# Router of a mixture-of-experts layer: the norm by tokens from turned blocks, its scale and shift behind the gather

## The chip, the core and the metric

The kernel runs on one core of a Trainium2 chip. The metric is device time in microseconds, the median of several runs. The engines named here are TensorE (PE), VectorE (DVE), ScalarE (ACT), GpSimd (POOL) and SyncE (SP), which issues the large weight transfers.

## The reference, cut to what matters

Two transformer blocks of two different kinds follow each other; the change lies in the first block's second layer, between its attention and its experts. There 256 tokens of width 1024 pass through:

```python
mix = jnp.concatenate([self_out, cross_out], axis=-1) @ w_out[i]
x = layer_norm(DN_ALPHA * x + mix, ln_attn_g[i], ln_attn_b[i])
ffn = moe_swiglu(x, w_router[j], b_router[j], w_exp_in[j], w_exp_out[j])
x = layer_norm(DN_ALPHA * x + ffn, ln_ffn_g[i], ln_ffn_b[i])
```

`moe_swiglu` takes `logits = x2 @ w_router + b_router`, the two largest of 8 logits for each token, a softmax of these two as gates, sends each token to its two experts (`silu(h[:, :D_FF]) * h[:, D_FF:]` between two linears) and adds the results up by the gates. `layer_norm` is `(x - mean) * rsqrt(var + eps) * g + b` over the 1024 features.

## The kernel before

Activations stand with features on the partitions: 8 blocks (`KB`) of 128 features by 256 tokens (`S`). A linear takes each weight tile from a 1 MB transfer (`raw`, issued by SP up to eight tiles ahead, five `raw` buffers and some borrowed ones); ACT makes the rounded upper part `wh` (L237), DVE the rest `wl = raw - wh` (L240), three buffers of each. Activations are split the same way (`xh`, `xl`, by `split`: ACT L218, DVE L219), and PE does three matmuls for each block of 128 by 128 weights: L285 (xh by wh), L286 (xl by wh), L287 (xh by wl). PSUM has four `acc` banks, two `pt` and two `sc`.

Each engine works its queue in the order in which the instructions stand. A tile framework's scheduler sets that order when the kernel is built: it takes what is ready by its own estimate, earlier written code first, and `tc.high_priority()` puts a piece ahead.

The second layer, in order of writing:

- `layer1` ends with the memory attention (exps L476, transposes L495, products L509, splits L218/L219). Then `residual` (L538) runs `w_out[1]`, 192 matmuls in four tiles, and evicts each of the 8 blocks on DVE as `z = alpha * x + p` (L543). `ln_mean` (L413) sums blocks on POOL and PE for the mean.
- `layer_norm` (L421): DVE subtracts the mean (L426), ACT squares (L410), PE sums the squares in 32 small matmuls (L429), `rsq` (L985 to L998) takes the inverse root on DVE, PE spreads it over the partitions (L436), DVE multiplies (L439), ACT applies scale and shift twice (L441 into `xh`, L442 into `z`), DVE makes `xl` (L444).
- `moe` (L733): starts the fetch of the first eight expert tiles, loads the router's weights `wr` on ACT's queue (`late`, L344), splits them, takes logits in 16 matmuls (L749), turns `z` into rows by tokens `xt` (transposes L758, splits L218/L219), turns the logits back (L762), picks the two experts (L768 to L785), counts positions (matmuls L789/L790, then L792/L793) and calls `gather` for the first two experts.
- `gather` (L839): one-hot matrices `oh` (L847), 32 matmuls with the upper and lower parts of `xt` into banks of their own (L854), copied out by ACT (L861, upper) and DVE (L859, lower) as `xe`, 128 by 512 each; then the turned one-hots (L868 to L873). It is called four times, the later three between expert linears.
- `expert_in` (L910 to L912) and `expert_out` run for 8 experts on tiles of 128 by 2048, then a conditional stage and the final norm.

Of the kernel before, what the change touches and what calls it, by code (L numbers as in the profile page):

```python
# [22 lines left out]
NM = 16  # L23
T2 = S + NM
# [5 lines left out]
ALPHA = 4.0 ** 0.25  # L30
# [134 lines left out]
class Kern:  # L165
# [372 lines left out]
    def residual(self, z, x, w, xs, alpha=ALPHA):  # L538
# [107 lines left out]
    def layer1(self, x, xh, xl):  # L646
        nc, I, tc = self.nc, self.i, self.tc
        with tc.tile_pool(name="l1", bufs=1) as pool:
            w = I["w_in_fox"][0]
# [10 lines left out]
            n = 0  # L660
# [53 lines left out]
        self.dbg("xa1", z)  # L714
        return z, xh, xl

    def log1p_exp_neg_abs(self, out, s, u, x):

# [11 lines left out]
        nc.vector.tensor_tensor(out, out, s, op=OP.mult)  # L730


    def moe(self, x, xh, xl):  # L733
        nc, I, tc = self.nc, self.i, self.tc
        c = self.c
        with tc.tile_pool(name="moe", bufs=1) as pool:

            raws = [None] * 5 + [self.idle(t) for t in ("xl", "xa")] + [self.pair_y(pool, F).rearrange("p a c -> p (a c)")]
# [3 lines left out]
            wr = self.late(pool, "wr")  # L742
            w2 = pool.tile([128, KB, 16], R, name="wr2")
            self.split(w2[:, :, :8], w2[:, :, 8:], wr)
            p = self.sc()[:16, :S]
            for k in range(KB):
                o = [(p, w2[:, k], xh[:, k]), (p[:8], w2[:, k, :8], xl[:, k])]
                for i, a in enumerate(o if k == 0 else o[::-1]):
                    nc.tensor.matmul(*a, start=k == 0 and i == 0, stop=k == KB - 1 and i == 1)  # L749
            lT = pool.tile([128, S], R, tag="ohT", name="ohT", bufs=3)[:16].bitcast(F)  # L750
            nc.scalar.activation(lT, p, AF.Copy)

            xt = [pool.tile([128, 2, D], R, name=f"xt{i}") for i in range(2)]
            for g in range(2):
                for t in range(2):
                    p = self.pt()
                    for b in range(4):
                        nc.tensor.transpose(p[:, ds(b * 128, 128)], x[:, g * 4 + b, ds(t * 128, 128)], self.ident)  # L758
                    self.split(*(a[:, t, ds(g * 512, 512)] for a in xt), p)
            p = self.sc()[:, :32].rearrange("p (t k) -> p t k", t=2)  # L760
            for t in range(2):
                nc.tensor.transpose(p[:, t], lT[:, ds(t * 128, 128)], self.ident[:16, :16])  # L762
            t8 = lambda name, dt=F, n=8: pool.tile([128, 2, n], dt, name=name)
            sel, gate, pos, lg, m8, ixf, e2 = (t8(n) for n in ("sel", "gate", "pos", "lg", "m8", "ixf", "e2"))
            ix, w4 = t8("ix", U32), t8("w4", n=4)
            b8 = lambda a: a.to_broadcast([128, 2, 8])
            tt = nc.vector.tensor_tensor
            tt(lg, p[:, :, :8], b8(self.brout[:, None, :]), op=OP.add)  # L768
            tt(lg, lg, p[:, :, 8:], op=OP.add)
            for t in range(2):  # L770
                nc.vector.max(m8[:, t], lg[:, t])
                nc.vector.max_index(ix[:, t], m8[:, t], lg[:, t])
            nc.vector.tensor_copy(ixf, ix)
            tt(w4[:, :, 0:1], m8[:, :, 1:2], m8[:, :, 0:1], op=OP.subtract)
            nc.scalar.activation(w4[:, :, 1:2], w4[:, :, 0:1], AF.Exp)
            nc.vector.tensor_scalar(w4[:, :, 2:3], w4[:, :, 1:2], 1.0, None, op0=OP.add)
            nc.vector.reciprocal(w4[:, :, 2:3], w4[:, :, 2:3])
            tt(w4[:, :, 3:4], w4[:, :, 1:2], w4[:, :, 2:3], op=OP.mult)
            i8 = b8(c["iota8"][:, None, :])
            tt(gate, i8, b8(ixf[:, :, 0:1]), op=OP.is_equal)  # L780
            tt(e2, i8, b8(ixf[:, :, 1:2]), op=OP.is_equal)
            tt(sel, gate, e2, op=OP.add)
            tt(gate, gate, b8(w4[:, :, 2:3]), op=OP.mult)
            tt(e2, e2, b8(w4[:, :, 3:4]), op=OP.mult)
            tt(gate, gate, e2, op=OP.add)  # L785
            p = self.sc()[:, :16].rearrange("p (t k) -> p t k", t=2)
            for t in range(2):
                if t:
                    nc.tensor.matmul(p[:, t], c["ones"], sel[:, 0], start=True, stop=False)  # L789
                nc.tensor.matmul(p[:, t], c["ustrict"], sel[:, t], start=t == 0, stop=True)  # L790

            nc.vector.scalar_tensor_tensor(pos, p, 1.0, sel, op0=OP.add, op1=OP.mult)  # L792
            nc.vector.tensor_scalar(pos, pos, -1.0, None, op0=OP.add)  # L793
            pg = lambda e: (pos[:, :, e:e + 1], gate[:, :, e:e + 1])
            pairs = lambda e: [pg(e), pg(e + 1)]
            got = self.gather(pool, xt, pairs(0), True)
            self.piece = 2048, 2048
# [41 lines left out]
    def gather(self, pool, xt, of, first=False):  # L839
# [7 lines left out]
                nc.vector.tensor_scalar(oh[:, t, ds(i * 128, 128)], c["iota"], pos[:, t], None, op0=OP.is_equal)  # L847
        xe = [self.ap_.tile([128, KB, T2], R, tag="xh", name="xe", bufs=2) for _ in range(2)]
        for b in range(0, KB, 2):
            for i in range(2):  # L850
                p = self.acc() if first else self.sc()
                for j in range(2):
                    for t in range(2):
                        nc.tensor.matmul(p[:, ds(j * w, w)], xt[i][:, t, ds((b + j) * 128, 128)], oh[:, t, :w],  # L854
                                         start=t == 0, stop=t == 1)
                o = xe[i][:, b:b + 2, :w]
                pv = p[:, :2 * w].rearrange("p (j t) -> p j t", j=2)
                if i:
                    nc.vector.tensor_copy(o, pv)  # L859
# [831 lines left out]
```

## Time and profile before

| | us |
|---|---|
| median of three runs | 2355.31 |
| lowest and highest of the three | 2350.05, 2355.98 |
| profiled execution, whole | 2352.28 |
| profiled execution, span of the profile | 2350.5 |
| PE busy in the span | 2266.5 (96%) |
| DVE busy | 1691.3 (72%) |
| ACT busy | 1324.2 (56%) |
| POOL busy | 63.1 (3%) |

The profile shows one execution. "Busy" of an engine is a share of time; which engine holds a stage is read from what waits for what. A row of the timeline has the start, the duration of the whole group, engine, line, operation, the names written and read, the shape, the count, and in brackets how long the engine was idle before it and what ended that. A row of a table by windows has the stretch, its length, each engine's busy time with the count of instructions, TensorE's granted clock (1.00 is full speed), the share of the DMA engines' time and GB/s.

### The profile page before, as it was taken

To read this page: it belongs to the slowest core of one execution; us is meant where nothing else is said; L and a number is where in the kernel's file an instruction comes from. 1 tells how busy PE (TensorE), PEld (TensorE's weight loads), DVE (VectorE), ACT (ScalarE), POOL (GpSimd) and SP (SyncE) were. 2 spreads that over 40 slices of the span, in tenths; PEclk is the share of its full clock that TensorE was granted. 3 is DMA by queue.
4 is the path that set the end of the run, shared out by engine and by line. 5 is a ranking of instruction groups with operands and counts; after the bars stand their busy time and mean duration, and the time that the engine had idled before them with its cause. 6 is when DMAs were issued, how large, how long until landed. Compare 5 with 4: busy or idle time off the path is not lost. (4 is left out here: it accounts for less than half of the span.)

```text
span 2350.5 us, 36949 instructions
## 1 busy us (share of the span) xinstructions
PE 2266.5 (96%) x14970; PEld 2018.7 (86%) x14970; DVE 1691.3 (72%) x2632; ACT 1324.2 (56%) x1836; POOL 63.1 (3%) x110
## 2 busy tenths in 40 slices
PE   8989998979999999999999779999999999999999
PEld 7679998768888888878888669989999989899999
DVE  6655547658888888888889656867776666758773
ACT  5454435447777766767767563455554563555552
POOL 0000000000000000000000000000000000000000
PEclk9799998979999999999999879999999989999999
DMA  7125554246999998999999412225445422244554
GB/s 284 62 91 187 181 183 143 90 145 252 357 339 338 364 338 330 359 348 346 340 356 359 169 54 77 91 92 177 156 170 174 148 77 90 73 144 158 191 185 131
DMA packets 70032, 478.91 MB, mean 204 GB/s; under 512 B 7960, under 2 KB 10906, under 8 KB 13792
## 3 DMA queue, kind: packets, MB, share of 16 engines
q1 hardware_dynamic: 68336, 475.08, 55.2%
q8 instruction: 119, 1.95, 0.3%
q10 hardware_dynamic: 1376, 1.29, 0.2%
q14 instruction: 57, 0.47, 0.1%
q0 software_dynamic: 144, 0.13, 0.0%
HBM read 475.55 MB, written 1.05 MB: 203 GB/s over the span
## 5 line engine op out<-in xcount | busy, mean ns | idle before, releaser
L240 DVE TENSOR_TENSOR wl<-raw,wh 128x1024 fp32r<-128x1024 f32 (+2 forms) x565 | 882.5, 1573 | 299.4 <-ACT wh L237 297.4
L237 ACT ACTIVATE wh<-raw 128x1024 fp32r<-128x1024 f32 (+2 forms) x565 | 744.8, 1332 | 416.0 <-PE acc L286 244.4
L285 PE MATMUL acc<-xh,wh 128*128 128x272 f32 (+2 forms) x2224 | 643.7, 292 | 3.5 <-ACT wh L237 1.8
L286 PE MATMUL acc<-xl,wh 128*128 128x272 f32 (+2 forms) x2224 | 645.3, 291 | 1.5 <-DVE xl L1048 1.2
L287 PE MATMUL acc<-xh,wl 128*128 128x272 f32 (+2 forms) x2224 | 641.1, 290 | 2.5 <-DVE wl L240 2.5
L285 PEld LDWEIGHTS acc<-xh,wh 128*128 128x128 f32 x2224 | 423.1, 191 | 11.9 <-ACT wh L237 3.0
L286 PEld LDWEIGHTS acc<-xl,wh 128*128 128x128 f32 x2224 | 423.4, 191 | 8.0 <-issue 4.4
L287 PEld LDWEIGHTS acc<-xh,wl 128*128 128x128 f32 x2224 | 423.6, 191 | 5.9 <-DVE wl L240 3.4
L912 PE MATMUL acc<-wl,xe 128*128 128x512 f32 (+1 forms) x768 | 289.2, 378 | 3.0 <-DVE wl L240 3.0
L910 PE MATMUL acc<-wh,xe 128*128 128x512 f32 (+1 forms) x768 | 289.2, 377 | 0.0
L911 PE MATMUL acc<-wh,xe 128*128 128x512 f32 (+1 forms) x768 | 289.1, 376 | 0.0
L240 DVE TENSOR_TENSOR wl<-rawxl,wh 128x2048 fp32r<-128x2048 f32 x73 | 166.4, 2289 | 17.9 <-ACT wh L237 17.6
L912 PEld LDWEIGHTS acc<-wl,xe 128*128 128x128 f32 x768 | 144.3, 188 | 31.3 <-DVE wl L240 5.1
L910 PEld LDWEIGHTS acc<-wh,xe 128*128 128x128 f32 x768 | 144.8, 189 | 27.0
L911 PEld LDWEIGHTS acc<-wh,xe 128*128 128x128 f32 x768 | 144.3, 188 | 26.0
L237 ACT ACTIVATE wh<-rawxl 128x2048 fp32r<-128x2048 f32 x73 | 139.6, 1916 | 32.1 <-PE acc L936 15.7
L285 PE MATMUL acc<-gh,wh 128*128 128x256 f32 (+1 forms) x528 | 150.3, 285 | 0.0
L286 PE MATMUL acc<-gl,wh 128*128 128x256 f32 (+1 forms) x528 | 150.3, 285 | 0.0
L287 PE MATMUL acc<-gh,wl 128*128 128x256 f32 (+1 forms) x528 | 150.1, 284 | 0.0
L936 PE MATMUL acc<-wh,egl 128*128 128x512 f32 x352 | 139.7, 397 | 0.0
L935 PE MATMUL acc<-wh,egh 128*128 128x512 f32 x352 | 139.0, 395 | 0.0
L937 PE MATMUL acc<-wl,egh 128*128 128x512 f32 x352 | 132.7, 395 | 0.0
(537 smaller groups left out, 2957.2 us busy)
## 6 DMA issues: line engine op xcount, KB each, us to landing
raw<-in_w_exp_in_dram SPq DMA_DIRECT2D x125, 1024.0 KB, 5.9
raw<-in_w_exp_out_dram SPq DMA_DIRECT2D x64, 1024.0 KB, 5.7
rawxl<-in_w_exp_in_dram SPq DMA_DIRECT2D x49, 1024.0 KB, 6.0
raw<-in_w_up_dram SPq DMA_DIRECT2D x44, 1024.0 KB, 4.8
rawxl<-in_w_exp_out_dram SPq DMA_DIRECT2D x24, 1024.0 KB, 6.5
raw<-in_w_in_dram SPq DMA_DIRECT2D x24, 1024.0 KB, 4.8
raw<-in_w_ffn_in_dram SPq DMA_DIRECT2D x22, 1024.0 KB, 4.8
raw<-in_w_out_dram SPq DMA_DIRECT2D x16, 1024.0 KB, 4.8
```

The lines of the kernel that those rows point to most:

```text
L237: nc.scalar.activation(h[:, o], raw[:, o], AF.Copy)
L240: nc.vector.tensor_tensor(l[:, o], raw[:, o], h[:, o].bitcast(F), op=OP.subtract)
L285: nc.tensor.matmul(o, f(wh[:, j]), xh[:, k], start=st, stop=False)
L286: nc.tensor.matmul(o, f(wh[:, j]), xl[:, k], start=False, stop=False)
L287: nc.tensor.matmul(o, f(wl[:, j]), xh[:, k], start=False, stop=sp)
L910: nc.tensor.matmul(a, xe[0][:, k], wh[:, q], start=k == 0, stop=False)
L911: nc.tensor.matmul(a, xe[1][:, k], wh[:, q], start=False, stop=False)
L912: nc.tensor.matmul(a, xe[0][:, k], wl[:, q], start=False, stop=k == KB - 1)
L935: nc.tensor.matmul(ys[h], gh[:, k], wh[:, q, o], start=k == 0, stop=False)
L936: nc.tensor.matmul(ys[h], gl[:, k], wh[:, q, o], start=False, stop=False)
L937: nc.tensor.matmul(ys[h], gh[:, k], wl[:, q, o], start=False, stop=k == FB - 1)
```

## The change

The residual of `w_out[1]` moves from the end of `layer1` into `moe`, behind new code that loads `wr` and forms from it, before any row is known: `gw = wr * g`, `bw = wr * b`, their sums over features `sb` (two DVE reductions and a matmul by ones), and adds the router's bias. `residual` gets a hook `done`: instead of `ln_mean`, each block k of the raw sum `z` is turned by two transposes into four banks (two `pt`, two `sc`) when the next one has been evicted, and DVE takes `bn_stats` of a bank when four blocks are in it. So mean and variance stand by tokens. Logits come from the raw sum in 16 matmuls with `gw` (plain f32) and are corrected by `r`, `-mean * r` and `sb`. ACT evicts the turned banks as normed rows (L791), which are split into `xt`. Scale and shift go into `gather`: upper and lower parts of `xt` accumulate in one bank, ACT (L902) or, for every other block of the first gather, DVE (L900) evicts 128 by 256 with scale and shift, and `split` (ACT L218, DVE L219) makes `xe`. The normed `z` that the final residual needs is made after the first gather is written: four matmuls that spread `r` (L828), 16 multiplies and adds on DVE (L832, L833), 8 scales and shifts on ACT (L834).

```diff
     def residual(self, z, x, w, xs, alpha=ALPHA, done=None):
         def ev(k, p):
             nc.vector.scalar_tensor_tensor(z[:, k], x[:, k], alpha, p, op0=OP.mult, op1=OP.add)
-            self.ln_mean(z, k, 6)
+            if done is None:
+                self.ln_mean(z, k, 6)
+            elif k:
+                done(k - 1)
...
+        if done:
+            done(KB - 1)
...
-        z = self.x_b()
-        self.residual(z, x, I["w_out"][1], (ah, al))
-        xh, xl = self.pair(S)
-        self.layer_norm(z, self.v["ln_attn_g"][:, 1], self.v["ln_attn_b"][:, 1], xh, xl)
-        return z, xh, xl
+        return x, ah, al
...
-    def moe(self, x, xh, xl):
+    def moe(self, x, ah, al):
+            wr = self.late(pool, "wr")
+            gw, bw = (pool.tile([128, KB, 8], F, name=n) for n in ("gw", "bw"))
+            tt(gw, wr, k8(g), op=OP.mult)
+            tt(bw, wr, k8(b), op=OP.mult)
+            sb = pool.tile([128, 2, 8], F, name="sb")
+            for i, a in enumerate((gw, bw)):
+                nc.vector.tensor_reduce(sb[:, i], a.rearrange("p k e -> p e k"), axis=AX.X, op=OP.add)
+            p = self.acc()[:, :16]
+            nc.tensor.matmul(p, c["ones"], sb.rearrange("p i e -> p (i e)"), start=True, stop=True)
+            nc.vector.tensor_copy(sb.rearrange("p i e -> p (i e)"), p)
+            tt(sb[:, 1], sb[:, 1], self.brout, op=OP.add)
+            z = self.x_b()
+            tp = [[f() for _ in range(2)] for f in (self.pt, self.sc)]
+            def turn(k):
+                for t in range(2):
+                    nc.tensor.transpose(tp[k // 4][t][:, ds(k % 4 * 128, 128)], z[:, k, ds(t * 128, 128)], self.ident)
+                if k % 4 == 3:
+                    with tc.high_priority():
+                        for t in range(2):
+                            nc.vector.bn_stats(st[:, t, k // 4], tp[k // 4][t])
+            self.residual(z, x, I["w_out"][1], (ah, al), done=turn)
...
-            w2 = pool.tile([128, KB, 16], R, name="wr2")
-            self.split(w2[:, :, :8], w2[:, :, 8:], wr)
...
+                pl = self.acc()[:, :16].rearrange("p (t e) -> p t e", t=2)
+                for t in range(2):
+                    for k in range(KB):
+                        nc.tensor.matmul(pl[:, t], z[:, k, ds(t * 128, 128)], gw[:, k], start=k == 0, stop=k == KB - 1)
...
+                    xn = pool.tile([128, 512], F, tag="eg", name="eg", bufs=2)
+                    nc.scalar.activation(xn, tp[q][t], AF.Identity, scale=r[:, t:t + 1], bias=r[:, 2 + t:3 + t])
+                    self.split(*(a[:, t, ds(q * 512, 512)] for a in xt), xn)
...
+            p = self.sc()
+            for i in range(4):
+                nc.tensor.matmul(p[:, ds(i * 128, 128)], r[:, i:i + 1].to_broadcast([128, 128]), self.ident,
+                                 start=True, stop=True)
+            x = z
+            for k in range(KB):
+                tt(z[:, k], z[:, k], p[:, :S], op=OP.mult)
+                tt(z[:, k], z[:, k], p[:, S:], op=OP.add)
+                nc.scalar.activation(z[:, k], z[:, k], AF.Identity, scale=g[:, k:k + 1], bias=b[:, k:k + 1])
...
+            for j in range(2):
+                k = b + j
+                xn = self.ap_.tile([128, T2], F, tag="sq", name="sq", bufs=2)[:, :w]
+                if first and j:
+                    nc.vector.tensor_scalar(xn, p[:, ds(j * w, w)], g, s, op0=OP.mult, op1=OP.add)
                 else:
-                    nc.scalar.activation(o, pv, AF.Copy)
+                    nc.scalar.activation(xn, p[:, ds(j * w, w)], AF.Identity, scale=g, bias=s)
+                self.split(xe[0][:, k, :w], xe[1][:, k, :w], xn)
```

In three places the engines' order shows it. First, PE's queue at the end of the attention. Before, matmuls of `w_out` (`acc<-xh,wh`) stand between the transposes (`pt<-cst,pe`) and products (`pt<-pT,vm`) of the last heads:

```order
L495 MATMUL pt<-cst,pe 128x128 x4
L285 MATMUL acc<-xh,wh 128x256 x4
L495 MATMUL pt<-cst,pe 128x128 x4
L509 MATMUL pt<-pT,vm_1428 64x256
L286 MATMUL acc<-xl,wh 128x256
L287 MATMUL acc<-xh,wl 128x256
L286 MATMUL acc<-xl,wh 128x256
L287 MATMUL acc<-xh,wl 128x256
L509 MATMUL pt<-pT,vm_1428 64x256 x3
```

The same place on PE now, up to the first matmuls of `w_out`:

```order
L464 MATMUL sc<-kmT_1115,qm 128x256 x3
L495 MATMUL pt<-cst,pe 128x128 x8
L509 MATMUL pt<-pT,vm_1428 64x256 x4
L495 MATMUL pt<-cst,pe 128x128 x8
L509 MATMUL pt<-pT,vm_1428 64x256 x4
L749 MATMUL acc<-sb,cst 128x16
L285 MATMUL acc<-xh,wh 128x256
L286 MATMUL acc<-xl,wh 128x256
```

All 192 matmuls of `w_out` have moved behind the attention and behind L749, the matmul by ones that reads `sb`. Second, DVE's queue behind the attention. Its last split of the attention is followed by the new code (`gw`, `bw`, `sb`), then by the rest `wl` of the third and fourth half tiles and by the evictions L543:

```order
L219 TENSOR_TENSOR xl<-pt,xh 128x256
L743 TENSOR_TENSOR gw<-wr,vec 128x64
L744 TENSOR_TENSOR bw<-wr,vec 128x64
L747 TENSOR_REDUCE sb<-gw 128x8
L747 TENSOR_REDUCE sb<-bw 128x8
L750 COPY sb<-acc 128x16
L751 TENSOR_TENSOR sb<-sb,vec 128x8
L240 TENSOR_TENSOR wl<-raw,wh 128x1024
L543 SCALAR_TENSOR_TENSOR xb<-xa,acc 128x256
```

Before, the evictions followed the split at once, and the router's weights `wr` were only split behind them:

```order
L219 TENSOR_TENSOR xl<-pt,xh 128x256
L543 SCALAR_TENSOR_TENSOR xb<-xa,acc 128x256 x4
L240 TENSOR_TENSOR wl<-raw,wh 128x2048
L219 TENSOR_TENSOR wr_5114<-wr,wr_5114 128x8x8
L543 SCALAR_TENSOR_TENSOR xb<-xa,acc 128x256
```

What the evictions and `w_out` stand behind has changed from the attention's last split to the arrival of `wr`. Third, DVE's queue at the start of the first expert, where `wl<-raw` are the expert's tiles, `xb<-xb,sc` is the late norm of `z`, and `sq`, `xe` belong to the gather:

```order
L886 TENSOR_SCALAR oh<-cst,pos 128x128
L833 TENSOR_TENSOR xb<-xb,sc 128x256
L832 TENSOR_TENSOR xb<-xb,sc 128x256
L240 TENSOR_TENSOR wl<-raw,wh 128x2048
L219 TENSOR_TENSOR xe<-sq,xe 128x256
L833 TENSOR_TENSOR xb<-xb,sc 128x256
L832 TENSOR_TENSOR xb<-xb,sc 128x256
L886 TENSOR_SCALAR oh<-cst,pos 128x128
L833 TENSOR_TENSOR xb<-xb,sc 128x256
```

Sixteen such multiplies and adds, and the last splits of the gather, now stand among the first expert's tiles, where before there were only tiles and the next one-hots.

## Rows read from the trace of the kernel before

**Rows 1.** Windows: stretch, length, PE, PEld, DVE, ACT, POOL busy, clock, DMA share, GB/s.

```profile
533.00:558.00 25.00, 25.00 (x112) 20.36 (x113) 19.44 (x20) 18.02 (x12) 0.00 (x0) 1.00 0.44 164
632.00:731.00 99.00, 99.00 (x488) 82.18 (x487) 86.37 (x62) 70.36 (x51) 0.00 (x0) 1.00 0.90 338
```

**Rows 2.** Waits of the expert stage, 560 to 1320: us in total, times, longest.

```profile
ACT wh L237 <- PE acc L911: 58.1, 70, 1.8
...
PEld acc L912 <- DVE wl L240: 5.1, 5, 1.0
```

**Rows 3.** Windows, matmuls of L285 alone, at the attention's end: PE, PEld, clock.

```profile
452.00:484.40 32.40, 7.95 (x31) 5.34 (x31) 1.00 0.19 63
```

**Rows 4.** Timeline of PE, one w_out matmul at a time (five left out).

```profile
484.98 0.28 PE L285 MATMUL acc<-xh,wh 128*128 128x256 f32 x1
...
485.69 0.28 PE L285 MATMUL acc<-xh,wh 128*128 128x256 f32 x1
```

**Rows 5.** Timeline of ACT in the last heads and behind the attention.

```profile
467.58 1.07 ACT L237 ACTIVATE wh<-raw 128x1024 fp32r<-128x1024 f32 x1
...
472.40 0.48 ACT L476 ACTIVATE pe<-sc,sm 128x256 f32<-128x256 f32 x1 [2.10 <-DVE sm L470]
...
482.29 0.38 ACT L218 ACTIVATE xh<-pt 128x256 fp32r<-128x256 f32 x1 [2.67 <-PE pt L509]
482.35 0.36 ACTq L344 DMA_DIRECT2D wr<-in_vec_dram  x1
```

**Rows 6.** DMA issues: KB each, us to landing.

```profile
wf<-in_vec_dram ACTq DMA_DIRECT2D x1, 48.0 KB, 1.8
wr<-in_vec_dram ACTq DMA_DIRECT2D x1, 32.0 KB, 5.1
```

**Rows 7.** Windows: the clock behind the residual and in the first layer's attention.

```profile
504.00:526.00 22.00, 13.35 (x53) 8.42 (x53) 12.75 (x53) 11.13 (x23) 0.00 (x0) 0.50 0.38 143
526.00:530.00 4.00, 3.67 (x17) 3.70 (x18) 1.47 (x5) 0.98 (x2) 0.00 (x0) 0.50 0.00 0
...
72.00:76.00 4.00, 2.01 (x12) 1.29 (x11) 3.42 (x14) 2.78 (x10) 0.00 (x0) 1.00 0.00 0
...
77.00:100.00 23.00, 23.00 (x72) 13.76 (x72) 10.43 (x47) 7.29 (x31) 0.00 (x0) 0.50 0.13 46
```

**Rows 8.** Timeline of DVE from the last eviction to the gather.

```profile
497.93 0.42 DVE L543 SCALAR_TENSOR_TENSOR xb<-xa,acc 128x256 f32<-128x256 f32 x1 [2.67 <-PE acc L287]
...
501.87 2.28 DVE L240 TENSOR_TENSOR wl<-raw,wh 128x2048 fp32r<-128x2048 f32 x1
...
507.37 0.16 DVE L998 SCALAR_TENSOR_TENSOR sm<-rqt,rqg 128x2 f32<-128x2 f32 x1
...
517.87 1.29 DVE L219 TENSOR_TENSOR xt<-pt,xt 128x512 fp32r<-128x512 f32 x2
...
523.70 0.18 DVE L782 TENSOR_TENSOR sel<-gate,e 128x16 f32<-128x16 f32 x1
...
525.48 0.17 DVE L792 SCALAR_TENSOR_TENSOR pos<-sc,sel 128x16 f32<-128x16 f32 x1 [1.24 <-PE sc L790]
...
525.89 0.88 DVE L847 TENSOR_SCALAR oh<-cst,pos 128x128 fp32r<-128x128 f32 x4
```

**Rows 9.** Timeline of PE: turning, gather, a small matmul's size, first expert.

```profile
513.90 0.63 PE L758 MATMUL pt<-cst,xb 128*128 128x128 f32 x2
...
526.43 5.72 PE L854 MATMUL acc<-oh,xt 128*128 128x256 f32 x32
...
532.10 0.50 PE L871 MATMUL sc<-gate,oh 128*128 128x1 f32 x4
...
533.08 0.48 PE L910 MATMUL acc<-wh,xe 128*128 128x512 f32 x1
```

**Rows 10.** Timeline of ACT: scale and shift of two blocks, the gather's eviction.

```profile
509.38 1.09 ACT L441 ACTIVATE xh<-xb,vec 128x256 fp32r<-128x256 f32 x2 [4.93 <-DVE xb L439]
...
531.72 0.60 ACT L861 ACTIVATE xe<-acc 128x512 fp32r<-128x512 f32 x1 [0.33 <-PE acc L854]
```

More of the change, by code (lines that the diff above doesn't have):

```diff
@@ L536, in mem_v, with residual @@
                     tokmajor=[(0, 256, lambda t, p: self.nc.vector.tensor_copy(self.vm[i][:, t], p))])
-    def residual(self, z, x, w, xs, alpha=ALPHA):
+    def residual(self, z, x, w, xs, alpha=ALPHA, done=None):
         nc = self.nc
@@ L736, in moe @@
         with tc.tile_pool(name="moe", bufs=1) as pool:
+            tt = nc.vector.tensor_tensor
+            g, b = (self.v[k][:, 1] for k in ("ln_attn_g", "ln_attn_b"))
+            wr = self.late(pool, "wr")
+            gw, bw = (pool.tile([128, KB, 8], F, name=n) for n in ("gw", "bw"))
+            k8 = lambda a: a[:, :, None].to_broadcast([128, KB, 8])
+            tt(gw, wr, k8(g), op=OP.mult)
[9 more added lines that the diff above has]
+            tp = [[f() for _ in range(2)] for f in (self.pt, self.sc)]
+            st = pool.tile([128, 2, 2, 6], F, name="st")
+            def turn(k):
[6 more added lines that the diff above has]
+            self.residual(z, x, I["w_out"][1], (ah, al), done=turn)
             raws = [None] * 5 + [self.idle(t) for t in ("xl", "xa")] + [self.pair_y(pool, F).rearrange("p a c -> p (a c)")]
@@ L740, in moe @@
             self.spare = True
-            wr = self.late(pool, "wr")
-            w2 = pool.tile([128, KB, 16], R, name="wr2")
-            self.split(w2[:, :, :8], w2[:, :, 8:], wr)
[L745 to L750, printed above, removed]
@@ L751, in moe @@
-            nc.scalar.activation(lT, p, AF.Copy)
+            with tc.high_priority():
+                pl = self.acc()[:, :16].rearrange("p (t e) -> p t e", t=2)
+                for t in range(2):
+                    for k in range(KB):
+                        nc.tensor.matmul(pl[:, t], z[:, k, ds(t * 128, 128)], gw[:, k], start=k == 0, stop=k == KB - 1)
+                mv = pool.tile([128, 2, 2], F, name="mv")
+                for t in range(2):
+                    nc.vector.bn_aggr(mv[:, t], st[:, t].rearrange("p g s -> p (g s)"))
+                v, r = self.small(2), self.small(4)
+                nc.vector.tensor_scalar(v, mv[:, :, 1], 1e-5, None, op0=OP.add)
+                self.rsq(r[:, :2], v)
+                nc.vector.scalar_tensor_tensor(r[:, 2:], mv[:, :, 0], -1.0, r[:, :2], op0=OP.mult, op1=OP.mult)
+                lg = pool.tile([128, 2, 8], F, name="lg")
+                for t in range(2):
+                    nc.vector.scalar_tensor_tensor(lg[:, t], pl[:, t], r[:, t:t + 1], sb[:, 1], op0=OP.mult, op1=OP.add)
+                    nc.vector.scalar_tensor_tensor(lg[:, t], sb[:, 0], r[:, 2 + t:3 + t], lg[:, t], op0=OP.mult, op1=OP.add)
@@ L753, in moe @@
             xt = [pool.tile([128, 2, D], R, name=f"xt{i}") for i in range(2)]
-            for g in range(2):
+            for q in range(2):
                 for t in range(2):
[L756 to L793, printed above, removed]
+                    xn = pool.tile([128, 512], F, tag="eg", name="eg", bufs=2)
+                    nc.scalar.activation(xn, tp[q][t], AF.Identity, scale=r[:, t:t + 1], bias=r[:, 2 + t:3 + t])
@@ new lines, in moe @@
+                    self.split(*(a[:, t, ds(q * 512, 512)] for a in xt), xn)
+            with tc.high_priority():
+                t8 = lambda name, dt=F, n=8: pool.tile([128, 2, n], dt, name=name)
+                sel, gate, pos, m8, ixf, e2 = (t8(n) for n in ("sel", "gate", "pos", "m8", "ixf", "e2"))
+                ix, w4 = t8("ix", U32), t8("w4", n=4)
+                b8 = lambda a: a.to_broadcast([128, 2, 8])
+                for t in range(2):
+                    nc.vector.max(m8[:, t], lg[:, t])
+                    nc.vector.max_index(ix[:, t], m8[:, t], lg[:, t])
+                nc.vector.tensor_copy(ixf, ix)
+                tt(w4[:, :, 0:1], m8[:, :, 1:2], m8[:, :, 0:1], op=OP.subtract)
+                nc.scalar.activation(w4[:, :, 1:2], w4[:, :, 0:1], AF.Exp)
+                nc.vector.tensor_scalar(w4[:, :, 2:3], w4[:, :, 1:2], 1.0, None, op0=OP.add)
+                nc.vector.reciprocal(w4[:, :, 2:3], w4[:, :, 2:3])
+                tt(w4[:, :, 3:4], w4[:, :, 1:2], w4[:, :, 2:3], op=OP.mult)
+                i8 = b8(c["iota8"][:, None, :])
+                tt(gate, i8, b8(ixf[:, :, 0:1]), op=OP.is_equal)
+                tt(e2, i8, b8(ixf[:, :, 1:2]), op=OP.is_equal)
+                tt(sel, gate, e2, op=OP.add)
+                tt(gate, gate, b8(w4[:, :, 2:3]), op=OP.mult)
+                tt(e2, e2, b8(w4[:, :, 3:4]), op=OP.mult)
+                tt(gate, gate, e2, op=OP.add)
+                p = self.acc()[:, :16].rearrange("p (t k) -> p t k", t=2)
+                for t in range(2):
+                    if t:
+                        nc.tensor.matmul(p[:, t], c["ones"], sel[:, 0], start=True, stop=False)
+                    nc.tensor.matmul(p[:, t], c["ustrict"], sel[:, t], start=t == 0, stop=True)
+                nc.vector.scalar_tensor_tensor(pos, p, 1.0, sel, op0=OP.add, op1=OP.mult)
+                nc.vector.tensor_scalar(pos, pos, -1.0, None, op0=OP.add)
@@ L796, in moe @@
             got = self.gather(pool, xt, pairs(0), True)
+            p = self.sc()
[7 more added lines that the diff above has]
+                nc.scalar.activation(z[:, k], z[:, k], AF.Identity, scale=g[:, k:k + 1], bias=b[:, k:k + 1])
+            self.dbg("xa1", z)
             self.piece = 2048, 2048
@@ L849, in gather @@
         for b in range(0, KB, 2):
-            for i in range(2):
-                p = self.acc() if first else self.sc()
-                for j in range(2):
+            p = self.acc() if first else self.sc()
+            for j in range(2):
+                for i in range(2):
                     for t in range(2):
                         nc.tensor.matmul(p[:, ds(j * w, w)], xt[i][:, t, ds((b + j) * 128, 128)], oh[:, t, :w],
[L855 to L859, printed above, removed]
-                else:
-                    nc.scalar.activation(o, pv, AF.Copy)
+                                         start=i == 0 and t == 0, stop=i == 1 and t == 1)
+            for j in range(2):
+                k = b + j
+                g, s = (self.v[n][:, 1, k:k + 1] for n in ("ln_attn_g", "ln_attn_b"))
+                xn = self.ap_.tile([128, T2], F, tag="sq", name="sq", bufs=2)[:, :w]
+                if first and j:
+                    nc.vector.tensor_scalar(xn, p[:, ds(j * w, w)], g, s, op0=OP.mult, op1=OP.add)
+                else:
+                    nc.scalar.activation(xn, p[:, ds(j * w, w)], AF.Identity, scale=g, bias=s)
+                self.split(xe[0][:, k, :w], xe[1][:, k, :w], xn)
         got = []
```

1 line of the change is left out of this document (removed).

## The prediction

> **What bounds the kernel now.** I read the table of windows first. In the expert stage PE is busy for 99 of 99 us at full clock, while DVE has 13 us and ACT 29 us to spare [rows 1]. The waits of the stage agree: ACT waits for PE's matmuls for 58.1 us, PE for a weight rest `wl` 5.1 us in five pieces [rows 2]. So from the first expert matmul on PE is the bound, with buffers full in front of it, and what delays or advances that matmul delays or advances the end one for one. The reader is to look at its start, 533.08 [rows 9]. The change acts on three stretches: what ends the residual (last eviction L543 at 497.93 + 0.42 = 498.35 [rows 8]), the chain from there to 533.08, which is 34.7 us, and the first expert, which gets new company on ACT and DVE.
>
> **Part 1: the residual is held.** In the last heads of the attention PE does `w_out` in the gaps: 31 matmuls of each of three kinds lie there [rows 3], with those that the trace lost about 96 of 192, half. One takes (485.69 - 484.98) / 6 = 0.118 us [rows 4]. In the new order all 192 stand behind L749, which reads `sb`, which is made from `wr`, and the load of `wr` is issued by ACT behind its last split of the attention, as before. So the free half is lost: 96 x 0.118 = 11.3 us come onto the path. Step by step:
> - The attention ends sooner. Two conversions of a half tile, 1.07 us each on ACT, stand in front of exps that ended a 2.10 us wait, and 96 matmuls in 32.4 us are 12, or 1.4 us, in PE's last 4 us, in which the last products stand behind them; together 2.1 + 1.4 = 3.5, of which I take 3.0, as not all lies in the chain (bounds 2 and 4.5, the latter with DVE's two rests as well). The load of `wr` is issued at 482.35 - 3.0 = 479.35 [rows 5].
> - `wr` landed 5.1 us after its issue [rows 6]: 484.45. It is issued beside a 1 MB expert tile now as before, so I take that; the lower bound is the 1.8 us of the 48 KB of `wf` [rows 6].
> - `gw`, `bw`, two reductions at 0.17 each (the small DVE instructions of [rows 8]) and the matmul by ones, 0.3: 1.0. `w_out` starts at 485.45.
> - 192 x 0.118 = 22.7. PE has then been idle for some 6 us, and after such a pause the clock is at half: the stretch behind the residual ran at 0.50, and came back only at 530, some 4 us into the gather, in which PE was busy for 3.67 of 4 us [rows 7]. Half of 4 us is lost: 2.0. So far 510.1.
> - Turning blocks: two transposes took 0.63 at half clock [rows 9], so 0.16 each at full: 14 before the last eviction, 2.2. Seven of the 16 logit matmuls stand there too; four instructions of a similar small matmul took 0.50 [rows 9], two instructions for one f32 matmul, so 0.25 each: 1.8.
> - The last eviction ends at 510.1 + 4.0 + 0.4 = 514.5, against 498.35: **+16.1**.
>
> Cover lost elsewhere: the sums on POOL and L419 that go were beside PE's work, worth nothing by themselves. If the clock falls already in the attention, it is rival C.
>
> One sentence on the load. The Trainium skill, "DMA: Bandwidth & Descriptors", section "Anatomy of one DMA — SWDGE (gpsimd) path", gives a DMA a fixed part of about 2.0 us plus its bytes over 436 GB/s; by that 32 KB land after an estimated 2.1 us and the sum is 3.0 us smaller. The 1.8 us of `wf` [rows 6] agree, the 5.1 us of `wr` itself don't, on a queue of ACT's (the page's fit is for GpSimd's).
>
> **Part 2: the chain to the first expert is shorter.** Removed: mean by L419, subtraction, squares, the 32 small matmuls of sums, the spread of `r`, L439 to L444, logits on split rows, the turn of the logits. What is left, from the last eviction:
> - nine logit matmuls at 0.25 and the last turn, 0.3: 2.6.
> - `bn_stats` of two banks, 128x512 out of PSUM; the nearest row is a split of that size, 1.29 for two [rows 8]: 1.3. Two aggregations 0.3.
> - An expert tile's rest, L240, 2.28, stands between the two aggregations on DVE; before it stood in the chain as well [rows 8]. 2.3.
> - Variance, ten of the root, one more: 12 x 0.17 = 2.0. Thirteen small instructions from the logits to `sel`, and two index loads: 2.4.
> - Prefix matmuls up to `pos`: 525.48 - 523.88 = 1.6; `pos` 0.4; two splits of `xt`, which now stand ahead of the one-hots, 1.3; one-hots 0.9 [rows 8].
> - Gather 5.7 [rows 9], at half clock for its first part as before; then 533.08 - 532.15 = 0.9 for the turned one-hots.
>
> Sum 21.7, so 514.5 + 21.7 = 536.2 for the first expert matmul: 34.7 - 21.7 = 13.0 gained, **-13.0**. ACT's evictions of normed rows (two of 128x256 took 1.09 [rows 10], so 1.1 for 128x512) and splits lie beside the DVE work. Bounds for the chain: 18 (the tile's rest slips out, splits are hidden) to 25.
>
> **Part 3: the first experts carry what was taken out.**
> - L828, four matmuls on a busy PE: **+0.5** (between 0.2 and 0.6).
> - 16 multiplies and adds at 0.42 (the size of L543 [rows 8]) on DVE, 6.7 us, and 8 scales and shifts at 0.55 [rows 10] on ACT, 4.4 us, among the first tiles; the gather's last splits, some 1 us each, come with them. The first 25 us hold 19.4 of DVE and 18.0 of ACT [rows 1]: 27.1 and 23.4 then, so DVE is 2 us over, and both keep to an order in which a tile waits behind this work. A PE stall of **+4.0**; bounds 0 (the three `wl` buffers cover it) and 7 (all of DVE's).
> - Three later gathers: ACT had 4 x 0.60 each [rows 10], and has 8 x 0.55 + 8 x 0.39 = 7.5 now; DVE changes by 0.7. That is 5.1 more ACT in a stage that has 0.29 of ACT free [rows 1]. Two `sc` banks come free later, so PE or a tile's `wh` can wait: 0.5 each, **+1.5**; bounds 0 and 6.
>
> Sum: 16.1 - 13.0 + 0.5 + 4.0 + 1.5 = **+9.1**. On the profiled execution, 2352.3 as a whole, that is 2361.4; that execution is 3.0 below the median, so the median forecast is 2355.3 + 9 = **2364**. A measurement here tells apart about 0.3%, 7.1 us: "same" is 2348.2 to 2362.4.
>
> **Rivals.**
> A. *The small costs vanish.* `wr` lands after 1.8 us (-3.3), and the first expert and the gathers absorb the added ACT and DVE work (-4.0 - 1.5). For it: DVE and ACT have 13 and 29 us of slack in 99. Against: the measured 5.1, and DVE over its time in the first 25 us. 9.1 - 8.8 = +0.3: **2356**, no change.
> B. *The shorter chain wins: faster.* Place: 479 to 536. Matmuls of `w_out` lie all along the last heads [rows 3], and if they held the chain up at several of them, not at the last alone, the attention ends 6 us sooner (the bound: half of the 11.3 us of `w_out` were in the way), not 3. With A and a chain of 18: 0.3 - 3.0 - 3.7 = -6.4; with no loss of clock -8.4. It decides from an attention 3 us shorter than I take, with A as well. **2347**. Against: exps wait for DVE and not for PE [rows 5].
> C. *The clock falls inside the attention.* Place: PE from 470 on. In the first layer's attention PE was busy 2.0 of 4 us and the next 23 us ran at 0.50 [rows 7]; without `w_out` the last heads here look like that. The rest of the attention on PE, an estimated 6 us at full clock behind 472 (10 us to its end less the waits and `w_out`), takes up to 6 longer and `w_out` starts no warmer: +5; with the gathers at their upper bound +4: **2373**. For it: that row. Against: exps and their waits set the pace there, so half of it may be covered.
> D. *The change doesn't do what it says for the path*: the `wr` load is taken early, `w_out` runs in the gaps again. The order excludes it, since PE takes L749 first; no chance of its own.
>
> **How the numbers follow.** Forecast 0.46 (its own range 2358 to 2370: 0.34 slower, 0.12 same); A 0.24 (0.03 faster, 0.21 same); B 0.11 (0.09 faster, 0.02 same); C 0.19 (all slower). Faster 0.12, same 0.35, slower 0.53. The range runs from 2350, where most of B is left out (0.09) and the lower rim of A is kept, to 2375, where a part of C with the upper bounds of part 3 is left out (0.08).
>
> **What would show it.** Part 1: the first `w_out` matmul at 484 to 487 and the last L543 near 514; wrong if L285 lies among the last heads or L543 ends before 509. The time from the issue of `wr` to its landing, 5.1 or 2, tells A's first half. Part 2: 20 to 24 us from there to the first matmul of the expert, which should start near 536. Part 3: PE's waits for `wl` or `wh` in the first 30 us of the experts, about 4 us, and in the windows of the three later gathers, half a microsecond each. C: a clock below 1.00 between 465 and 485. The forecast is wrong as a whole if the expert stage starts before 530, or if it starts at 536 and still ends by the old time, which would mean that PE's order there is not the bound.

## Result and profile after

The changed kernel takes 2370.36 us (median of 4 runs, 2367.37 to 2372.47), the kernel before 2353.40 beside it: ratio 1.0072, 95% interval 1.0060 to 1.0085, slower by 17 us. The forecast was slower by 9, 2364, in a range of 2350 to 2375. The direction and the main cause held; two steps were wrong by some 4 and 6 us. Single executions of one kernel differ: the kernel before, unaltered, took from 2349.16 to 2369.99 us in 28 executions beside c1, longer where the granted clock of the whole was lower (0.97 to 0.96).

The span of the profile is 2370.7 us, against 2350.5. Marks that both kernels share divide it: an exp (ACT L476) of an earlier pair of heads, at 423.68 before; the attention's last split on ACT; the end of the last eviction (DVE L543); the first expert matmul; the end of the experts' last matmul of the output linear (`wl,egh`). All later runs are read by the same marks, and each row is one execution:

| kernel | to the exp | attention to last split | to last eviction | chain to first expert | experts | behind them | span |
|---|---|---|---|---|---|---|---|
| before | 423.7 | 58.6 | 16.1 | 34.7 | 791.4 | 1026.0 | 2350.5 |
| before, again (c3) | 425.6 | 59.9 | 16.1 | 34.7 | 791.4 | 1023.9 | 2351.6 |
| changed | 427.5 | 59.2 | 35.1 | 20.1 | 796.7 | 1032.1 | 2370.7 |
| changed, again (c1) | 424.3 | 60.8 | 35.2 | 20.2 | 796.7 | 1032.1 | 2369.3 |
| e1 sums behind the residual | 424.7 | 58.6 | 15.4 | 22.4 | 796.7 | 1032.3 | 2350.2 |
| e2 hold alone | 424.8 | 59.2 | 33.5 | 34.9 | 791.4 | 1027.8 | 2371.5 |
| e3 late norm | 423.1 | 62.6 | 34.5 | 19.9 | 793.1 | 1032.0 | 2365.1 |
| e4 idle matmuls in the attention | 425.3 | 56.1 | 34.5 | 19.8 | 796.7 | 1028.4 | 2360.8 |
| e5 sums behind, late norm | 423.2 | 58.6 | 15.9 | 18.7 | 793.0 | 1031.7 | 2341.2 |
| e5 again (c2) | 424.9 | 58.6 | 15.9 | 20.2 | 793.2 | 1030.1 | 2342.8 |

The first column is code that no version alters: its 3.8 us between `before` and `changed` are chance (423.1 to 427.5 over all). Without them the change adds 0.6 + 19.0 - 14.6 + 5.3 + 6.1 = 16.4 us.

**The hold.** First ACT and DVE, then PE of the changed kernel at the attention's end (timeline; columns as in [rows 5]):

```profile
486.66 0.38 ACT L218 ACTIVATE xh<-pt 128x256 fp32r<-128x256 f32 x1 [1.81 <-PE pt L509]
486.72 0.36 ACTq L344 DMA_DIRECT2D wr<-in_vec_dram  x1
...
491.98 0.23 DVE L743 TENSOR_TENSOR gw<-wr,vec 128x64 f32<-128x64 f32 x1 [4.48 <-DMA wr<-in_vec_dram]
...
492.44 0.25 DVE L747 TENSOR_REDUCE sb<-bw 128x8 f32<-128x64 f32 x1
...
521.32 0.42 DVE L543 SCALAR_TENSOR_TENSOR xb<-xa,acc 128x256 f32<-128x256 f32 x1 [1.62 <-PE acc L287]
```

```profile
484.91 1.72 PE L509 MATMUL pt<-pT,vm 128*64 128x256 f32 x8
492.79 0.58 PE L749 MATMUL acc<-sb,cst 128*128 128x16 f32 x2 [6.17 <-issue]
493.21 0.56 PE L285 MATMUL acc<-xh,wh 128*128 128x256 f32 x1
```

The load is issued behind the last split as before ([rows 5]), lands 5.2 us later, and PE stands idle for 6.17 us until L749. The profile names no cause for that wait (`issue`), but L749 starts 0.10 us behind the end of the last reduction (L747), whose result it reads. Then all of `w_out` follows, 28.5 us from its first matmul to the last eviction. That is step by step what was forecast, except where it starts: 493.2, not 485.5.

**The clock in the attention.** Windows of the kernel before (stretch, length, PE busy, granted clock, DMA share, GB/s), then of the changed one (all engines, as in [rows 1]):

```profile
456.00:470.00 14.00, 14.00 (x86) 1.00 0.00 0
470.00:482.30 12.30, 10.04 (x66) 1.00 0.25 87
```

```profile
455.00:460.00 5.00, 3.15 (x21) 2.02 (x21) 2.88 (x14) 1.89 (x9) 0.00 (x0) 1.00 0.48 197
460.00:465.00 5.00, 3.27 (x11) 1.66 (x9) 2.65 (x11) 1.93 (x8) 0.00 (x0) 0.53 0.01 3
465.00:470.00 5.00, 5.00 (x16) 2.79 (x16) 2.77 (x9) 1.06 (x3) 0.00 (x0) 0.50 0.00 0
```

With `w_out` among the heads the clock is 1.00 (2.4 GHz) throughout these windows. Without it PE is busy for some 3 us of 5, the clock falls to 0.50 (1.2 GHz), and PE's transposes and products, now slow, fill the next stretch.

**The chain.** DVE from the last blocks' statistics to the one-hots, then PE (timeline of the changed kernel):

```profile
524.17 1.30 DVE L763 BATCH_NORM_STATS2 st<-sc 128x6 f32<-128x512 f32 x2 [2.43 <-PE sc L759]
...
525.49 2.24 DVE L240 TENSOR_TENSOR wl<-raw,wh 128x2048 fp32r<-128x2048 f32 x1
...
529.74 0.35 DVE L784 SCALAR_TENSOR_TENSOR lg<-acc,sm,sb 128x8 f32<-128x8 f32 x2
...
531.39 0.17 DVE L810 TENSOR_TENSOR sel<-gate,e 128x16 f32<-128x16 f32 x1
...
534.80 0.87 DVE L886 TENSOR_SCALAR oh<-cst,pos 128x128 fp32r<-128x128 f32 x4
```

```profile
521.79 2.17 PE L773 MATMUL acc<-gw,xb 128*128 128x8 f32 x18 [0.30 <-DVE xb L543]
...
535.33 5.61 PE L893 MATMUL acc<-oh,xt 128*128 128x256 f32 x32
...
541.87 0.47 PE L952 MATMUL acc<-wh,xe 128*128 128x512 f32 x1
```

20.1 us where the table of [rows 8] and [rows 9] had 34.7; the expert tile's rest (L240) stands in it, as forecast.

**The first expert.** Windows of 40 us from the first expert matmul on, before and changed (columns as in [rows 1]), and the waits of the changed kernel there:

```profile
533.10:573.10 40.00, 40.00 (x180) 32.51 (x180) 32.68 (x27) 28.73 (x20) 0.00 (x0) 1.00 0.64 236
```

```profile
542.00:582.00 40.00, 37.48 (x167) 29.34 (x167) 36.52 (x46) 31.18 (x30) 0.00 (x0) 1.00 0.52 198
```

```profile
PEld acc L954 <- DVE wl L240: 3.5, 3, 2.0
...
PE acc L954 <- DVE wl L240: 2.2, 3, 1.6
```

PE, never idle there before, is idle for 2.5 us, waiting for `wl` while DVE works through the late norm.

### The profile page after: what moved, and what is told of

It reads as the page before. It is cut to its first block, busy times and chain, and to the rows that moved or that the text cites. A ratio compares the mean times of both kernels' runs of the same rounds, so it can differ in the third digit from the quotient of the medians.

```text
span 2370.7 us, 36970 instructions
## 1 busy us (share of the span) xinstructions
PE 2272.1 (96%) x14950; PEld 2025.0 (85%) x14950; DVE 1694.2 (71%) x2658; ACT 1332.5 (56%) x1866; POOL 57.3 (2%) x105
## 3 DMA queue, kind: packets, MB, share of 16 engines
HBM read 475.55 MB, written 1.05 MB: 201 GB/s over the span
## 5 line engine op out<-in xcount | busy, mean ns | idle before, releaser
L240 DVE TENSOR_TENSOR wl<-raw,wh 128x1024 fp32r<-128x1024 f32 (+2 forms) x565 | 881.7, 1572 | 302.2 <-ACT wh L237 300.5
L285 PE MATMUL acc<-xh,wh 128*128 128x272 f32 (+2 forms) x2224 | 648.0, 294 | 2.7 <-ACT xh L441 1.1
L285 PEld LDWEIGHTS acc<-xh,wh 128*128 128x128 f32 x2224 | 426.4, 193 | 10.0 <-issue 2.4
L240 DVE TENSOR_TENSOR wl<-rawxl,wh 128x2048 fp32r<-128x2048 f32 x73 | 166.4, 2289 | 17.2 <-ACT wh L237 17.1
L285 PE MATMUL acc<-gh,wh 128*128 128x256 f32 (+1 forms) x528 | 150.3, 285 | 0.0
```

The costliest lines, as they stand in the source:

```text
L240: nc.vector.tensor_tensor(l[:, o], raw[:, o], h[:, o].bitcast(F), op=OP.subtract)
L285: nc.tensor.matmul(o, f(wh[:, j]), xh[:, k], start=st, stop=False)
```

## Experiments

**The changed kernel again (c1)**, unaltered.

> The changed kernel once more, unaltered, as the yardstick for the other runs beside it. Its first profile gave, against the kernel before: +3.8 us ahead of the change (first layer, same order of instructions), +0.6 in the attention, +19.0 from the issue of wr to the last eviction, -14.6 in the chain to the first expert matmul, +5.3 in the expert stage, +6.1 behind the experts (same order of instructions). Theory 1: the +3.8 and +6.1 are chance, from where the clock's half-speed stretches fall; then they change here by some us and the three middle terms stay within 1 us. Theory 2: they belong to the change (the code's place, the clock's history); then they come again, +3 to +4 and +5 to +7. Time 2367 to 2372 in either case.

2369.05 us. The middle terms came again (the attention within 1.6 us). The +3.8 ahead of the change did not (424.3): chance. The +6 behind the experts did, so theory 1 fell for that term; it gets runs of its own below.

**The hold undone (e1).**

```
-            wr = self.late(pool, "wr")
...
-            tt(sb[:, 1], sb[:, 1], self.brout, op=OP.add)
             z = self.x_b()
...
             self.residual(z, x, I["w_out"][1], (ah, al), done=turn)
+            wr = self.late(pool, "wr")
...
+            tt(sb[:, 1], sb[:, 1], self.brout, op=OP.add)
```

> Undoes the hold alone: the load of wr, gw, bw, their sums and the matmul by ones are written behind the residual instead of ahead of it; everything else of the change stays. In the built order matmuls of w_out lie among the last heads again. Theory 1 (the hold is what costs): the attention ends as before the change and at full clock, the last eviction comes 16 to 20 us sooner than in the changed kernel, the chain gets 2 us longer since all 16 logit matmuls now stand behind the last eviction, so 2352 to 2356 in all, about the kernel before. Theory 2 (the loss is in the expert stage and the gathers; w_out has slack anyway): 2366 to 2371, the expert stage starts sooner but nothing comes of it.

2350.99 us beside 2369.05 for c1 and 2353.11 for the kernel before (ratio to that 0.9987, 0.9966 to 1.0008): the hold's 18 us are gone (the time is 1 us under theory 1's range). The attention is back at 58.6, the clock at its end too, and the last eviction 15.4 us behind the last split. The chain grew by 2.3, as all 16 logit matmuls now stand in it (windows of PE, then PE's timeline):

```profile
455.00:470.00 15.00, 15.00 (x94) 1.00 0.00 1
...
498.48 4.56 PE L773 MATMUL acc<-gw,xb 128*128 128x8 f32 x32
```

Since e1 keeps the rest of the change, theory 2 (the expert stage takes any gain back) falls: its expert stage starts 19 us sooner than in c1 and is just as long.

**The hold alone (e2)**, in the kernel before:

```
-        z = self.x_b()
-        self.residual(z, x, I["w_out"][1], (ah, al))
...
+            wr = self.late(pool, "wr")
+            sb = self.small(8)
+            nc.vector.tensor_reduce(sb, wr.rearrange("p k e -> p e k"), axis=AX.X, op=OP.add)
+            p = self.acc()[:, :8]
+            nc.tensor.matmul(p, c["ones"], sb, start=True, stop=True)
+            nc.vector.tensor_copy(sb, p)
+            z = self.x_b()
+            self.residual(z, x, I["w_out"][1], (ah, al))
```

> Does the hold alone: the kernel before, with its own norm, router and gather, but the residual of w_out moved into the expert part behind the load of wr, a reduction over it and a matmul by ones whose result nobody uses. Theory 1 (the hold costs some 16 us plus 3.6 for the clock in the attention): 2371 to 2376, as the shorter chain is missing; half clock in the last heads. Theory 2 (the hold costs little by itself): 2354 to 2360.

2372.81 us, 19.7 above the kernel before (ratio 1.0068, 1.0038 to 1.0097): theory 1. DVE, PE and a window of PE in the last heads:

```profile
489.09 0.27 DVE L736 TENSOR_REDUCE sm<-wr 128x8 f32<-128x64 f32 x1 [4.27 <-DMA wr<-in_vec_dram]
...
489.42 0.60 PE L738 MATMUL acc<-sm,cst 128*128 128x8 f32 x2 [5.36 <-DVE sm L736]
489.87 0.56 PE L285 MATMUL acc<-xh,wh 128*128 128x256 f32 x1
...
457.00:472.00 15.00, 12.63 (x49) 0.66 0.00 1
```

Here the profile names DVE's reduction as what ends PE's wait. To the last eviction it takes 33.5 us instead of 16.1; the chain and the experts are as before. Up to the experts' end the hold alone adds 18.1 us and the whole change 10.3; the two times, 2372.81 and 2369.05, aren't separated by their intervals.

**The clock in the attention (e4).** The changed kernel, with matmuls that nobody needs in the gaps that `w_out` left:

```
         c = self.c
+        p = self.acc()
+        for _ in range(96):
+            nc.tensor.matmul(p[:, :256].rearrange("p (j t) -> p j t", j=2), self.identb,
+                             self.causb[:, None, :].to_broadcast([128, 2, 128]), start=True, stop=True)
         with tc.tile_pool(name="moe", bufs=1) as pool:
```

> The changed kernel plus 96 idle matmuls (128x128 by 256 columns, result unused) written ahead of the load of wr; the built order strews them among the last heads, where w_out's matmuls stood in the kernel before. The hold of w_out stays. Theory 1 (without w_out PE is idle enough in the last heads that the clock falls to half, which costs 2 to 4 us there): the clock stays at 1.00 from 452 to the last split, and the attention, from its first exps of the fourth pair of heads on to the last split, takes 56 to 58.6 us, not 59.2 to 62.6 as in the three profiles with the hold; the time falls by 2 to 4 us, to 2365 to 2367. Theory 2 (the attention waits for DVE and ACT, and the half clock is hidden): 59 us and more, no change of the time.

Windows of PE, c1 and then e4, over the same heads:

```profile
455.00:470.00 15.00, 12.78 (x42) 0.54 0.00 1
470.00:485.00 15.00, 11.82 (x51) 0.77 0.00 0
```

```profile
457.00:471.00 14.00, 13.96 (x87) 1.00 0.00 1
471.00:481.80 10.80, 10.61 (x79) 1.00 0.01 2
```

With idle work the clock stays up and the attention takes 56.1 us: 3.1 to 6.5 less than in the four profiles with the hold (59.2 twice, 60.8, 62.6), and 2.5 less than with `w_out` among the heads (58.6), close to the forecast's -3.0 for what no longer stands in its way. The mean granted clock from the exp to the last split orders the stretch in the profiles of the table: with the hold 56.1 us at 1.00, 59.2 at 0.86 (twice), 60.8 at 0.83 and 62.6 at 0.78; with `w_out` among the heads 58.6 at 1.00 and 59.9 at 0.97 (c3). The time, 2363.27, is 2 us under theory 1's range, and the stretch behind the experts, 3.7 us shorter here than in c1 at the same code, has a part in that; its ratio to the kernel before, 1.0050 (1.0032 to 1.0069), doesn't separate it from c1 (1.0054, 1.0035 to 1.0074), so this rests on the stretch, not on the total.

**The late norm (e3).** The spreading matmuls, multiplies, adds, scales and shifts of `z`:

```
             got = self.gather(pool, xt, pairs(0), True)
-            p = self.sc()
...
-                nc.scalar.activation(z[:, k], z[:, k], AF.Identity, scale=g[:, k:k + 1], bias=b[:, k:k + 1])
...
                 gT = self.expert_in(pool, now[0], I["w_exp_in"][e])
+                if e == 0:
+                    p = self.sc()
...
+                        nc.scalar.activation(z[:, k], z[:, k], AF.Identity, scale=g[:, k:k + 1], bias=b[:, k:k + 1])
```

> The changed kernel with the norm of z for the final residual (four spreading matmuls, 16 multiplies and adds, 8 scales and shifts) written behind the first expert's input linear instead of ahead of it, so that it no longer stands among that expert's first tiles. Theory 1 (these steps make PE wait there for 2.5 us): PE's waits for wl and wh in the first 40 us of the expert stage fall from 5 to 6 us in PE and weight load records to under 1.5, and the time by 2 to 3 us, 2367 to 2369 where the changed kernel shows 2370. Theory 2 (the gather's splits, not the norm, are late there): no change of the waits, within 1 us.

Windows of the first 40 us of its experts:

```profile
540.00:580.00 40.00, 40.00 (x182) 32.38 (x182) 34.12 (x34) 30.05 (x24) 0.00 (x0) 1.00 0.61 227
```

PE is never idle, and the expert stage takes 793.1 instead of 796.7: theory 1, 3.6 us for the place of the norm, of which 2.5 were PE's idle time. The total (2367.49 beside 2369.05, ratios 1.0051 and 1.0054) doesn't separate it from c1. The 1.7 us that remain over 791.4 are L828 (eight records, 1.05 us in the changed kernel) and the three later gathers together; PE has six waits of 0.6 us for a `wl` in e3's expert stage and five before. A gather alone wasn't tried.

**Both repaired (e5, c2).** Sums behind the residual (the load and `gw`, `bw` stay ahead), the late norm, and the transposes of `turn` under `tc.high_priority()`, so that they pass the logit matmuls.

> The changed kernel with three places of its order altered: the matmul by ones and what follows it written behind the residual (so w_out lies among the last heads again; the load of wr, gw and bw stay ahead), the norm of z for the final residual written behind the first expert's input linear, and the blocks' transposes put ahead of the logit matmuls. Nothing is left out. Theory: the single effects add up, the undone hold -18, the late norm -3.6 in the expert stage, the transposes -1 to -2 in the chain: first expert matmul at 519 to 521, expert stage 793, 2344 to 2348, 0.2 to 0.4% faster than the kernel before. Rival: the expert stage gives the sooner start back (the transfers of weights or the added ACT work bind): 2350 to 2354.

> The combined kernel once more, as the yardstick for the run with the idle matmuls on the same chip: expert stage 793, 1031 to 1033 us behind it, 2344 to 2347.

2345.55 us, ratio to the kernel before 0.9976 (0.9962 to 0.9989); again 2344.72, 0.9957 (0.9939 to 0.9974): faster than the kernel before by 7 to 9 us of median, and than the changed one (c1) by some 24 (18 to 23 by the ratios). PE of e5, its last turn, its gather and its first expert matmul:

```profile
498.76 0.42 PE L755 MATMUL sc<-cst,xb 128*128 128x128 f32 x2
...
510.25 5.23 PE L895 MATMUL acc<-oh,xt 128*128 128x256 f32 x32
...
516.42 0.49 PE L954 MATMUL acc<-wh,xe 128*128 128x512 f32 x1
```

The effects add up; the rival (the sooner start is given back) falls. The first expert matmul comes 3 us sooner than expected. In c2, the same program, the chain took 20.2 us instead of 18.7: its gather took 6.63 us at a mean granted clock of 0.56, that of e5 5.23 at 0.75.

**Behind the experts.** Instructions stand there in the same order in all versions, yet the stretch took 1032 us in both profiles of the changed kernel and 1026.0 and 1023.9 in the two of the kernel before. Matmuls nobody needs were put into the first expert of the kernel *before* (23, 15 and 7 of 512 columns: e6, e7, e9):

```
             got = self.gather(pool, xt, pairs(0), True)
+            p = self.sc()
+            for _ in range(23):
+                nc.tensor.matmul(p.rearrange("p (j t) -> p j t", j=4), self.identb,
+                                 self.causb[:, None, :].to_broadcast([128, 4, 128]), start=True, stop=True)
```

> The kernel before with 23 idle matmuls of 512 columns (0.232 us each, 5.3 us, result unused) in the first expert. All four profiles with the changed expert stage (796.7 us, or 793.1 in the one with the late norm) show 1032 us behind the experts, in code whose order is the same; the two without it show 1026 and 1028. Theory 1 (the length of the expert stage alone decides where the clock's fall behind it comes, and that decides how much of the next stage runs at half): expert stage 796.7, behind it 1031 to 1033, 2363 to 2366 in all. Theory 2 (something of the changed code itself is felt there): 796.7 and 1026 to 1028, 2358 to 2360.

> The same with 15 idle matmuls, 3.5 us. Theory 1 as it reads from the profiles: the clock's fall then comes as in the kernel before, 7.5 to 8 us behind the experts' last matmul or a step earlier, and the stage behind the experts takes 1026 to 1028; 2356 to 2359 in all. Theory 3 (any lengthening of the expert stage costs 5 us more behind it): 1031 to 1033, 2361 to 2364.

> The kernel before with 7 idle matmuls of 512 columns in the first expert, 1.6 us. With 5.3 us the stage behind the experts took 1033.4, with 3.5 us 1024.2, with none 1026.0. Theory 1: a length between none and 3.5 us takes the same way as the changed kernel, 1030 to 1033; theory 3 (each lengthening costs in proportion): 1026 to 1028.

> The kernel before once more, for a second profile. Theory 1 (the stage behind the experts is set by where the clock's half-speed stretches fall, which in this kernel comes out the same each time): 1025 to 1029 us behind the experts, and a mean granted clock there as in the first profile. Theory 4 (it is chance from run to run): anything from 1024 to 1033.

Experts 796.3, 794.7, 792.8 and 791.4; behind them 1033.3, 1024.2, 1029.6 and 1023.9; times 2364.25 (ratio 1.0054, 1.0037 to 1.0072), 2356.13 (1.0016, 1.0007 to 1.0025), and single executions of 2356.96 and 2353.37. So the long stretch appears without any changed code, and more added work can cost less. The medians say the same: e6 is 11.4 us above the kernel before (2352.89) for 4.9 us more in the experts, e7 3.2 for 3.3. Theories 2 and 3 fall. Theory 1 isn't shown either: e7, e9 and c3 lie outside its ranges, and e4 has 1028.4 behind the changed kernel's 796.7 us of experts. Theory 4, chance from one execution to the next, stays open, as the nine executions of e6 alone run from 2358.19 to 2373.89. Windows of PE over 110 us from the experts' last matmul, in the kernel before, the changed one, e6 and e7:

```profile
1324.50:1384.50 60.00, 39.17 (x233) 0.74 0.30 105
1384.50:1434.50 50.00, 44.65 (x327) 0.90 0.22 73
```

```profile
1338.60:1398.60 60.00, 39.42 (x218) 0.69 0.29 103
1398.60:1448.60 50.00, 44.65 (x275) 0.76 0.20 69
```

```profile
1330.30:1390.30 60.00, 38.24 (x209) 0.69 0.29 103
1390.30:1440.30 50.00, 44.65 (x270) 0.76 0.20 69
```

```profile
1331.40:1391.40 60.00, 38.68 (x229) 0.74 0.29 103
1391.40:1441.40 50.00, 44.65 (x327) 0.90 0.21 73
```

The stretch goes with the granted clock: 0.74 and 0.90 where it is short, 0.69 and 0.76 where it is long. Over the whole stretch the mean is 0.97 in its two shortest profiles (1023.9 and 1024.2) and 0.96 in all of 1028 us and more. What decides where the clock falls wasn't found, as the last run of this kind shows: five such matmuls (1.2 us) in e5.

> The combined kernel (sums behind the residual, late norm, transposes first) plus 5 idle matmuls of 512 columns in the first expert, 1.2 us of work that nobody uses. Theory 1 (the length of the expert stage decides where the clock's fall behind it lies; 5.3 and 3.5 us more in the kernel before gave 1033.4 and 1024.2 us behind the experts where it has 1026.0): the fall moves from 6 us behind the experts' last matmul to between 7 and 8, the stage behind takes 1024 to 1027 instead of 1031.7, and the kernel gets faster by 3.5 to 6 us through added work, 2340 to 2343. Theory 2 (the 5 us belong to the changed code): slower by 1.2 us, 2346 to 2348.

2343.76 beside 2344.72 for c2: neither theory's time. Its profile has 1030.1 us behind the experts, as c2 itself had; the added work cost nothing that can be measured, and gained nothing. Inconclusive.

## Why the prediction was nearly right

- **What bounds the kernel**: right up to the experts' end. In e1 an expert stage that starts sooner ends sooner by as much, and in e5 by as much and the 3.6 us of the late norm. Behind it the later start wasn't all: the stretch that follows grew by itself, as told below.
- **Part 1, the hold**: right in kind and size. Landing of `wr` 5.2 (5.1 taken); from its issue to `w_out` 6.5 (6.1); from there to the last eviction 28.5 (29.1). Rival A's first half, a load of 1.8 us, fell. So did the 2.1 us estimated from the Trainium skill, "DMA: Bandwidth & Descriptors", section "Anatomy of one DMA — SWDGE (gpsimd) path": the measured 5.2, on a queue of ACT's, decides.
- **The attention 3.0 sooner**: wrong, +0.6 to +4.0 with the hold. This is the step that failed: the gain was there (2.5 us in e4's one profile, where the clock is held), but the half clock took 3.1 to 6.5 us back, and the sum had nothing for it. Rival C's mechanism belonged into the sum. The row of the first layer's attention showed it, and the argument against it (exps and their waits set the pace) did not carry. That the time, 2370, lies nearer to rival C's 2373 than to the forecast's 2364 is luck in part: C's 4 us for the gathers didn't come, and the loss behind the experts was in no rival.
- **Part 2**: -14.6, forecast -13.0; no single term explains the 1.6 us. The logit matmuls were sized right (18 instructions in 2.17 us, 0.24 a matmul, 0.25 taken). The small DVE instructions from the logits to `sel` took 1.8 us (2.4), and the gather started 0.5 us behind the start of the one-hots (0.9 taken); the rest is spread over the others, 0.1 or 0.2 each.
- **Part 3**: +5.3, forecast +6.0; right in sum, unevenly split: 3.6 for the place of the norm (4.0), 1.7 for L828 and the gathers (2.0).
- **Behind the experts**: no term at all in the sum, +6.1. Nothing was moved there, and the prediction took the later start to pass on one for one. The stretch went with the granted clock; whether the change or chance put the clock's fall there stays open, though the medians of the changed kernel and the kernel before, 17.0 and 15.9 us apart, have room for these 6 us beside the 10.3 up to the experts' end.

The two misses, 3.6 (3.1 of it the clock by e4's 56.1, 0.5 the size of the gain) and 6.1, less 0.1 (hold), 1.6 (chain) and 0.7 (experts), make the 7.3 us between 9.1 and 16.4; the medians differ by 17.0. The range held the result because it was wide enough for one rival's price, not because these terms were in it.

## What to carry to other kernels

A step whose input comes by a small late load must not stand ahead, in an engine's queue, of work that was filling other work's gaps: look in the built order for what it holds back, and write it behind. Work that fills gaps on TensorE pays twice, once for itself and once for the clock of what it fills; count the stretch at both levels of the clock when it goes. Work taken off a critical chain is not gone: put it where its engine has slack, here one linear later.

## What the runs showed of the hardware

- Code in the same order took from 1023.9 to 1033.3 us behind the experts, 0.9%, longer where the granted clock was lower; this is more than several of the effects studied. Stretches of a profile, not totals, separate effects of 3 us, and a stretch in which the clock falls differs by 1.3 to 1.5 us at the same code (the attention 58.6 and 59.9, the chain of e5 and c2 18.7 and 20.2).
- Adding 96 matmuls without use to the attention made that stretch 3.1 to 6.5 us shorter; its granted clock was 1.00 with them and 0.86 to 0.78 without.
- A load of 32 KB landed 5.1 to 5.3 us after its issue in each of the nine profiles that show it (before, c3, changed, c1, e3, e4, e6, e7, e9), in four of them (changed, c1, e3, e4) with PE idle behind it.
